# High and low input in one 512-column matmul, in half chunks of 256 channels

## The chip, the cores and the metric

The kernel runs on one core of a Trainium2 chip. The metric is the device time of one execution in microseconds. TensorE (PE) multiplies, with its weight loads (PEld) beside it; VectorE (DVE) and ScalarE (ACT) do the elementwise work; GpSimd (POOL) and SyncE (SP) issue most of the DMAs.

## The reference, cut to what matters

Two layers over x of 256 tokens by 2048 channels. Each layer projects x by `w_in` to 7680 columns, which three mixers share; the mixers' outputs are gated, joined, projected by `w_out` and merged into x.

```python
proj = x @ w_in
aq, ak, av, ag, bq, bk, bv, bg, cu, cglu, cg = jnp.split(proj, IN_OFFSETS, axis=-1)
ya = diff_attention(aq, ak, av, bias_a, lam, ...) * silu(ag)      # 4 heads of 128
yb = dilated_attention(bq, bk, bv, bias_b) * silu(bg)             # 8 heads of 128
yc = conformer_conv(cu, cglu, ...) * silu(cg)                     # 512 channels, 31 taps
x = layer_norm(ALPHA * x + jnp.concatenate([ya, yb, yc], -1) @ w_out, ln_g, ln_b)
```

All of it is float32.

## The kernel before, in words

**Products.** TensorE multiplies in its rounded float32 format. To keep the precision, every factor is split in a high part (the value rounded) and a low part (the remainder), and a product is the sum of three: high by high, high by low, low by high (`mm3`, lines 220 to 223). x^T lies in SBUF as `xh` and `xl`, [128 channels, 16 k-tiles, 256 tokens] each.

**Weights.** The columns of `w_in`, `conv_pw` and `w_out` come in groups of 512 KB, either 2 k-tiles by 512 columns (rows of 2 KB in DRAM) or 4 k-tiles by 256 columns (rows of 1 KB). `Stream` (lines 104 to 167) loads them into 5 `wraw` buffers by DMAs from SP, and splits each: ACT copies the high part (line 154), DVE subtracts for the low part (line 155). There are 6 buffers for each part. `pump`, called after each group, issues the next split as soon as the count of buffers allows with a slack of one, so a split waits for TensorE to be done with a group five places ahead of it.

**Chunks.** A layer's projection runs in chunks of 512 columns, 8 groups each. Twelve of them (cglu, cu, ag, aq, ak, bg, bq, bk, bg, bq, bk, cg) come out with channels on partitions: `chunk_w` (line 225) takes the weights as the stationary operand, 128 columns at a time (4 blocks `b`), and streams 256 tokens, so a k-tile is 4 x 3 matmuls of 256 columns. The others (av, bv) and the output projection come out with tokens on partitions: `chunk_x` (line 241) takes x as the stationary operand and streams 512 weight columns. Both sum in `acc`, 4 KB per partition of PSUM, of which there are two.

**The way out.** `evac` copies `acc` to SBUF on ACT, with a scale where wanted. `gate` takes ACT's tanh of `acc` and then a DVE step that reads `acc` again. For ak, two ACT copies put the two partition halves into `kz`. For cglu and cu, tanh on ACT and a DVE product into `hpad`.

**Fillers.** All other work of the layer is cut in steps and hung on ticks (`at`, `tick`); one tick passes after each k-tile of a dense chunk. The 124 taps of the convolution per layer (line 473, DVE) start at the chunk ag, at first one on each tick; heads of the attentions (`a_head`, `b_head`) run their scores, softmax, transposes and outputs on fixed ticks, among them small matmuls in TensorE's queue. Engines work through their queues in the order of the program.

Of the kernel before, what the change touches and what calls it, by code (L numbers as in the profile page):

```python
# [9 lines left out]
F32 = mybir.dt.float32  # L10
# [6 lines left out]
S = 256  # L17
# [4 lines left out]
CW = 31  # L22
# [19 lines left out]
def kernel(  # L42
# [32 lines left out]
    def u4(name, dt=F32):  # L75
        return work.tile([128, 1024], dt, tag="u4", name=name, bufs=N_U4)
# [3 lines left out]

    xh = big.tile([128, KT, S], F32R, name="xh")
    xl = big.tile([128, KT, S], F32R, name="xl")
    yh = big.tile([128, KT, S], F32R, name="yh")
# [16 lines left out]

# [1 line left out]
    groups = []  # L102

    class Stream:
# [33 lines left out]
        def split_part(self, i):  # L138
            """The two parts of group 0, which arrive one by one."""
            if i == 0:  # L140
                self.tiles(0)
            r, h, l = self.raw[0][:, i], self.hi[0][:, i], self.lo[0][:, i]
            nc.scalar.copy(h, r)
            nc.vector.tensor_tensor(l, r, h.bitcast(F32), OP.subtract)
            if i == 1:
                self.raw.pop(0)
                self.ns = 1
# [35 lines left out]
    for l in range(DEPTH):  # L183
        p = {}
        w = w_in[l]
        if l == 0:
            p["av"] = add_groups(w, OFF["av"], 512, KALL, 2)
        else:
            p["av0"] = add_groups(w, OFF["av"], 256, KALL, 4)
            p["av1"] = add_groups(w, OFF["av"] + 256, 256, KALL, 4)  # L190
        for c, o in (("cglu", 0), ("cu", 0), ("ag", 0), ("aq", 0), ("ak", 0),
                     ("bv", 0), ("bg", 0), ("bq", 0), ("bk", 0),
                     ("bv", 512), ("bg", 512), ("bq", 512), ("bk", 512), ("cg", 0)):
            p[c, o // 512] = add_groups(w, OFF[c] + o, 512, KALL, 2)
        p["pw"] = add_groups(conv_pw[l], 0, 512, list(range(4)), 2)
        for n in range(3):
            p["o", n] = add_groups(w_out[l], n * 512, 512, KOUT0 if n == 0 else KALL, 2)
        p["o3a"] = add_groups(w_out[l], 1536, 256, KALL, 4)
        p["o3b"] = add_groups(w_out[l], 1792, 256, KALL, 4)
        plan.append(p)  # L200

# [1 line left out]
    ticks = deque()  # L203
# [14 lines left out]

# [1 line left out]
    def mm3(o, ah, al, bh, bl, start, stop, skip=False):  # L220
        nc.tensor.matmul(out=o, lhsT=ah, rhs=bh, start=start, stop=False, skip_group_check=skip)  # L221
        nc.tensor.matmul(out=o, lhsT=ah, rhs=bl, start=False, stop=False, skip_group_check=skip)  # L222
        nc.tensor.matmul(out=o, lhsT=al, rhs=bh, start=False, stop=stop, skip_group_check=skip)  # L223

    def chunk_w(ids, mh, ml, nk=KT):
# [32 lines left out]
    def half_steps(ids, mh, ml, t, o, gi):  # L258
        """The products of one token tile with one group of a 256-column half."""
        ts = slice(t * 128, (t + 1) * 128)  # L260
# [5 lines left out]

# [1 line left out]
    def stage_y(kt, y):  # L268
# [6 lines left out]
    def b_head(h, q, k, v, g, t0):  # L275
        """Stages of one head of mixer B; h is its number, q, k, v, g its chunk's tiles."""
        j = h % 4
# [157 lines left out]

# [1 line left out]
    def gate(acc, name):  # L437
        t = u4(name)
        tv = v4(t, 4)
        nc.scalar.activation(tv, acc, AF.Tanh, scale=0.5)  # L440
        nc.vector.scalar_tensor_tensor(tv, tv, 1.0, acc, OP.add, OP.mult)
        return tv

    def evac(acc, name, scale=None):
        t = v4(u4(name), 4)
        if scale is None:
            nc.scalar.copy(t, acc)
        else:
            nc.scalar.activation(t, acc, AF.Copy, scale=scale)
        return t  # L450

# [4 lines left out]

# [1 line left out]
    def conv_start(l, acc_u, tg):  # L458
        """hpad <- 2 * cu * sigmoid(cglu); tg holds tanh(cglu / 2)."""
        nc.vector.scalar_tensor_tensor(hpad[:, :, CW - 1:], tg, 1.0, acc_u, OP.add, OP.mult)  # L460

# [86 lines left out]

# [1 line left out]
    class Norm:  # L550
        """r holds alpha * x + y by column chunk: [128 tokens, 2 token tiles, 512]."""

# [21 lines left out]
        def add(self, t, h, ps):  # L574
            """Column half h (256 wide) of token tile t."""
            r = self.r[h // 2][:, t, (h % 2) * 256:(h % 2 + 1) * 256]
            nc.vector.scalar_tensor_tensor(r, r, ALPHA, ps, OP.mult, OP.add)
            nc.vector.bn_stats(self.bn[t][:, h, :], r)
# [41 lines left out]

# [1 line left out]
    xr = [v4(u4("xr"), 4) for i in range(4)]  # L622
# [97 lines left out]

# [1 line left out]
    def enter(N, step):  # L722
        """Layer norm into x^T, the first chunk's products by token tile between: step(t, gi)."""
        def norm(t, *ns):
# [52 lines left out]

# [1 line left out]
    prev = None  # L779
    for l in range(DEPTH):  # L780
# [3 lines left out]
        else:  # L784
# [19 lines left out]
            av = avt  # L804
        acc = chunk_w(P["cglu", 0], xh, xl)
        tg = v4(u4("tg"), 4)
        nc.scalar.activation(tg, acc, AF.Tanh, scale=0.5)
        acc = chunk_w(P["cu", 0], xh, xl)
        conv_start(l, acc, tg)
        cd = {}  # L810
# [8 lines left out]
        conv_tail(l, cd, 166)  # L819
        ag = gate(chunk_w(P["ag", 0], xh, xl), "ag")  # L820
        aq = evac(chunk_w(P["aq", 0], xh, xl), "aq", 1.0 / 8.0)
        acc = chunk_w(P["ak", 0], xh, xl)
        nc.scalar.copy(kz[0:64, :, 0, :], acc[0:64])
        nc.scalar.copy(kz[64:128, :, 1, :], acc[64:128])
        for h in range(AH):
            a_head(l, h, aq, av, ag, 1 + 15 * h)
        sB = float(HD) ** -0.5
        for c in range(2):
            bv = evac_v(chunk_x(P["bv", c], xh, xl, KALL), "bv")
            bg = gate(chunk_w(P["bg", c], xh, xl), "bg")  # L830
            bq = evac(chunk_w(P["bq", c], xh, xl), "bq", sB)
            bk = evac(chunk_w(P["bk", c], xh, xl), "bk")
            for h in range(4):
                b_head(4 * c + h, bq, bk, bv, bg, 1 + (15 if c == 0 else 6) * h)
        acc = chunk_w(P["cg", 0], xh, xl)
        cg = gate(acc, "cg")
        acc = chunk_w(P["pw"], cd["hh"], cd["hl"], nk=4)
        for b in range(4):
            y = ytile()
            nc.vector.scalar_tensor_tensor(y, acc[:, b, :], 0.25, cg[:, b, :], OP.mult, OP.mult)  # L840
            stage_y(12 + b, y)
        # output projection
        N = Norm(l)
# [60 lines left out]
def _shape_consts():  # L904
    """One-hot buckets and window masks per distance 255 - m, and the identity and its mirror: functions of the shapes alone."""
    import numpy as np
# [46 lines left out]
```

## Time and profile before

| | us |
|---|---|
| median of 3 runs | 958.03 |
| lowest and highest of them | 957.79, 958.13 |
| span of the profiled execution, first to last instruction | 956.7 |
| TensorE busy | 936.8 |
| DVE busy | 636.5 |
| ACT busy | 438.2 |

The profile gives the profiled execution by its span alone. A busy TensorE is not TensorE at its peak: matmuls overlap, and the profile models their ends. The spacing of their starts tells what one costs in a stream. PEclk is the granted share of TensorE's full clock, in tenths.

### The profile page before, as it was taken

Reading aid. Unit: us, or ns where it says so; the run is one execution under the profiler, and the core shown is the slowest. Engines: PE = TensorE matmul, PEld = TensorE weight load, DVE = VectorE, ACT = ScalarE, POOL = GpSimd, SP = SyncE. Lnnn points to the kernel's source line nnn. Section 1 sums busy time; section 2 is a strip of 40 time slices with the busy share of each in tenths; the row PEclk is TensorE's granted clock in tenths of the full one; section 3 lists DMA queues with packets and bytes.
Section 4 is the critical chain, followed back from the end, with each engine's and each line's share of the span. In section 5 each row is a group of like instructions: output and inputs, shape, how many; then the busy total and the mean of one; then the engine's idle time right before and its main releaser. Section 6 shows DMA issues by size and latency. Waiting matters only on the chain. (4 is left out here: it accounts for less than half of the span.)

```text
span 956.7 us, 16597 instructions
## 1 busy us (share of the span) xinstructions
PE 936.8 (98%) x6710; PEld 881.0 (92%) x6710; DVE 636.5 (67%) x1030; ACT 438.2 (46%) x623; POOL 58.1 (6%) x78
## 2 busy tenths in 40 slices
PE   7999999999999999999999999999999999999995
PEld 5999998999999999888989999989998999998894
DVE  5657777676767567656765477767776676766556
ACT  5553345454544456433354433455455444654331
POOL 2100000000000000200240000000000000010004
PEclk9999999999999999999999999999999999999998
DMA  9956665555665555976457666665656655568632
GB/s 319 336 161 189 186 181 175 158 173 155 182 180 165 170 163 177 297 231 192 139 202 238 180 182 190 178 176 156 176 156 175 177 168 163 163 224 285 199 99 88
DMA packets 96285, 179.44 MB, mean 188 GB/s; under 512 B 5928, under 2 KB 18496, under 8 KB 96208
## 3 DMA queue, kind: packets, MB, share of 16 engines
q1 hardware_dynamic: 92096, 165.17, 56.4%
q0 software_dynamic: 3824, 12.68, 4.4%
q8 instruction: 52, 0.85, 0.4%
q10 hardware_dynamic: 288, 0.52, 0.1%
q14 instruction: 25, 0.20, 0.1%
HBM read 174.14 MB, written 4.21 MB: 186 GB/s over the span
## 5 line engine op out<-in xcount | busy, mean ns | idle before, releaser
L155 DVE TENSOR_TENSOR wlo<-wraw,whi 128x1024 fp32r<-128x1024 f32 x307 | 374.4, 1223 | 210.9 <-ACT whi L154 209.8
L154 ACT CAST whi<-wraw 128x1024 fp32r<-128x1024 f32 x307 | 320.5, 1049 | 296.7 <-PE acc L222 166.0
L221 PE MATMUL acc<-xh,whi 128*128 128x256 f32 x1536 | 442.2, 288 | 0.0
L223 PE MATMUL acc<-xh,wlo 128*128 128x256 f32 x1536 | 434.6, 283 | 0.0
L222 PE MATMUL acc<-xl,whi 128*128 128x256 f32 x1536 | 434.5, 283 | 0.0
L221 PEld LDWEIGHTS acc<-xh,whi 128*128 128x128 f32 x1536 | 294.6, 192 | 2.1 <-issue 1.4
L222 PEld LDWEIGHTS acc<-xl,whi 128*128 128x128 f32 x1536 | 294.5, 192 | 2.1 <-issue 1.4
L223 PEld LDWEIGHTS acc<-xh,wlo 128*128 128x128 f32 x1536 | 294.3, 192 | 0.0
L473 DVE SCALAR_TENSOR_TENSOR cacc<-hpad,cwh,cacc 128x256 f32<-128x256 f32 x240 | 115.4, 481 | 2.4
L221 PE MATMUL acc<-whi,yh 128*128 128x512 f32 (+1 forms) x256 | 93.8, 366 | 0.0
L223 PE MATMUL acc<-whi,yl 128*128 128x512 f32 (+1 forms) x256 | 92.9, 363 | 0.0
L222 PE MATMUL acc<-wlo,yh 128*128 128x512 f32 (+1 forms) x256 | 92.8, 363 | 0.0
L221 PE MATMUL acc<-whi,xh 128*128 128x512 f32 (+1 forms) x192 | 74.1, 386 | 1.6 <-ACT whi L154 1.0
L222 PE MATMUL acc<-wlo,xh 128*128 128x512 f32 (+1 forms) x192 | 71.9, 375 | 2.0 <-DVE wlo L155 1.5
L223 PE MATMUL acc<-whi,xl 128*128 128x512 f32 (+1 forms) x192 | 71.8, 374 | 0.0
L223 PEld LDWEIGHTS acc<-whi,yl 128*128 128x128 f32 x256 | 48.3, 189 | 7.7
L222 PEld LDWEIGHTS acc<-wlo,yh 128*128 128x128 f32 x256 | 48.4, 189 | 7.5
L221 PEld LDWEIGHTS acc<-whi,yh 128*128 128x128 f32 x256 | 48.3, 189 | 7.3
L221 PEld LDWEIGHTS acc<-whi,xh 128*128 128x128 f32 x192 | 36.2, 189 | 10.0 <-ACT whi L154 1.8
L222 PEld LDWEIGHTS acc<-wlo,xh 128*128 128x128 f32 x192 | 36.2, 189 | 9.3 <-DVE wlo L155 2.1
L223 PEld LDWEIGHTS acc<-whi,xl 128*128 128x128 f32 x192 | 36.2, 188 | 6.6
L410 POOL TENSOR_TENSOR sa<-sa,mhalf 128x2 f32<-128x2 f32 x8 | 5.8, 725 | 431.4 <-DVE sa L409 431.4
(175 smaller groups left out, 661.1 us busy)
## 6 DMA issues: line engine op xcount, KB each, us to landing
wraw<-in_w_in_dram SPq DMA_DIRECT2D x239, 512.0 KB, 4.3
wraw<-in_w_out_dram SPq DMA_DIRECT2D x64, 512.0 KB, 4.9
wraw<-in_conv_pw_dram SPq DMA_DIRECT2D x4, 512.0 KB, 4.4
rt<-in_x_dram POOLq DMA_DIRECT2D x4, 512.0 KB, 6.9
gb<-in_ln_g_dram POOLq DMA_DIRECT2D x8, 256.0 KB, 7.3
gb<-in_ln_b_dram POOLq DMA_DIRECT2D x8, 256.0 KB, 8.1
x_mid<-rt POOLq DMA_DIRECT2D x8, 256.0 KB, 7.1
rt<-x_mid POOLq DMA_DIRECT2D x4, 512.0 KB, 7.1
```

Of the source, the lines that this page charges most:

```text
L154: nc.scalar.copy(h, r)
L155: nc.vector.tensor_tensor(l, r, h.bitcast(F32), OP.subtract)
L221: nc.tensor.matmul(out=o, lhsT=ah, rhs=bh, start=start, stop=False, skip_group_check=skip)
L222: nc.tensor.matmul(out=o, lhsT=ah, rhs=bl, start=False, stop=False, skip_group_check=skip)
L223: nc.tensor.matmul(out=o, lhsT=al, rhs=bh, start=False, stop=stop, skip_group_check=skip)
L410: nc.gpsimd.tensor_tensor(m[:, 24:26], m[:, 22:24], mhalf[:, 0:2], OP.pow)
L473: nc.vector.scalar_tensor_tensor(a, h, w, a, OP.mult, OP.add)
```

## The change: what it does

- `xh` and `xl` become the two halves of one tile `xx`, [128, 16, 2, 256], so that the high and the low input of a k-tile lie side by side.
- The twelve chunks with channels on partitions run in two halves of 256 columns each. Their weights come in groups of 4 k-tiles by 256 columns, in rows of 1 KB.
- In `half_w`, for each k-tile and block, one matmul streams `xx[:, k]`, 512 columns, past the high weights into two parts of `acc` (high input, low input), and one of 256 columns streams the high input past the low weights into the second part. A tick passes after every second k-tile.
- `whole` sums the two parts on the way out: ACT copies the second part to SBUF, DVE adds the first from PSUM. `gate` works on that sum, with tanh and product on later ticks; `evac`, `conv_start` and `kz` use `whole` too.

The core of the diff (lines that only lose a comment are left out):

```diff
-    xh = big.tile([128, KT, S], F32R, name="xh")
-    xl = big.tile([128, KT, S], F32R, name="xl")
+    xx = big.tile([128, KT, 2, S], F32R, name="xx")
+    xh, xl = xx[:, :, 0, :], xx[:, :, 1, :]
...
-            p[c, o // 512] = add_groups(w, OFF[c] + o, 512, KALL, 2)
+            if c == "bv":
+                p[c, o // 512] = add_groups(w, OFF[c] + o, 512, KALL, 2)
+            else:
+                p[c, o // 512] = [add_groups(w, OFF[c] + o + 256 * j, 256, KALL, 4) for j in range(2)]
...
+    def half_w(ids, m2, nk=KT):
+        acc = acc_tile().rearrange("p (b i) s -> p b i s", b=2)
+        k = 0
+        for g in ids:
+            wh, wl = st.get(g)
+            for kk in range(nk // len(ids)):
+                for b in range(2):
+                    cs = slice(b * 128, (b + 1) * 128)
+                    nc.tensor.matmul(out=acc[:, b], lhsT=wh[:, kk, cs], rhs=m2[:, k], start=k == 0, stop=False,
+                                     skip_group_check=True)
+                    nc.tensor.matmul(out=acc[:, b, 1], lhsT=wl[:, kk, cs], rhs=m2[:, k, 0], start=False,
+                                     stop=k == nk - 1, skip_group_check=True)
+                k += 1
+                if k % 2 == 0:
+                    tick()
+            st.done(g)
+            st.pump()
+        return acc
...
-    def gate(acc, name):
-        t = u4(name)
-        tv = v4(t, 4)
-        nc.scalar.activation(tv, acc, AF.Tanh, scale=0.5)
-        nc.vector.scalar_tensor_tensor(tv, tv, 1.0, acc, OP.add, OP.mult)
+    def whole(z, acc, scale=None, c=slice(0, 128)):
+        if scale is None:
+            nc.scalar.copy(z, acc[c, :, 1])
+            nc.vector.tensor_tensor(z, acc[c, :, 0], z, OP.add)
+        else:
+            nc.scalar.activation(z, acc[c, :, 1], AF.Copy, scale=scale)
+            nc.vector.scalar_tensor_tensor(z, acc[c, :, 0], scale, z, OP.mult, OP.add)
+
+    def gate(ids, m2, name):
+        tv = v4(u4(name), 4)
+        for j in range(2):
+            z = tv[:, 2 * j:2 * j + 2, :]
+            whole(z, half_w(ids[j], m2))
+            d = {}
+
+            def s0(z=z, d=d):
+                d["t"] = work.tile([128, 768], F32, tag="s", name="s", bufs=3)[:, 0:512].rearrange(
+                    "p (b s) -> p b s", b=2)
+                nc.scalar.activation(d["t"], z, AF.Tanh, scale=0.5)
+
+            def s1(z=z, d=d):
+                nc.vector.scalar_tensor_tensor(z, d["t"], 1.0, z, OP.add, OP.mult)
+
+            at(1, s0)
+            at(2, s1)
         return tv
 
-    def evac(acc, name, scale=None):
...
+    def evac(ids, m2, name, scale=None):
+        tv = v4(u4(name), 4)
+        for j in range(2):
+            whole(tv[:, 2 * j:2 * j + 2, :], half_w(ids[j], m2), scale)
+        return tv
...
-        nc.vector.scalar_tensor_tensor(hpad[:, :, CW - 1:], tg, 1.0, acc_u, OP.add, OP.mult)
+    def conv_start(l, P):
+        tg = v4(u4("tg"), 4)
+        for j in range(2):
+            z = tg[:, 2 * j:2 * j + 2, :]
+            whole(z, half_w(P["cglu", 0][j], xx))
+            nc.scalar.activation(z, z, AF.Tanh, scale=0.5)
+        for j in range(2):
+            z = hpad[:, 2 * j:2 * j + 2, CW - 1:]
+            whole(z, half_w(P["cu", 0][j], xx))
+            nc.vector.scalar_tensor_tensor(z, tg[:, 2 * j:2 * j + 2, :], 1.0, z, OP.add, OP.mult)
...
-        acc = chunk_w(P["ak", 0], xh, xl)
-        nc.scalar.copy(kz[0:64, :, 0, :], acc[0:64])
-        nc.scalar.copy(kz[64:128, :, 1, :], acc[64:128])
+        ag = gate(P["ag", 0], xx, "ag")
+        aq = evac(P["aq", 0], xx, "aq", 1.0 / 8.0)
+        for j in range(2):
+            acc = half_w(P["ak", 0][j], xx)
+            for c in range(2):
+                ps = slice(64 * c, 64 * c + 64)
+                whole(kz[ps, 2 * j:2 * j + 2, c, :], acc, c=ps)
```

`bg`, `bq`, `bk` and `cg` change in the same way. `chunk_w` stays for `conv_pw` alone.

## Rows read from the trace of the kernel before

**Rows 1.** The page: busy time of each engine, and granted clock in 40 slices
```profile
PE 936.8 (98%) x6710; PEld 881.0 (92%) x6710; DVE 636.5 (67%) x1030; ACT 438.2 (46%) x623; POOL 58.1 (6%) x78
...
PEclk9999999999999999999999999999999999999998
```

**Rows 2.** Waits of TensorE and its weight loads, whole span (total, times, longest)
```profile
PE acc L264 <- ACT xh L615: 2.2, 3, 1.4
...
PE acc L264 <- DVE xl L619: 0.3, 1, 0.3
...
PEld acc L221 <- issue: 2.6, 9, 0.6
...
PEld aux L321 <- ACT pt L315: 0.7, 2, 0.3
```

**Rows 3.** Groups by line and shape: busy us, mean ns | idle before
```profile
L221 PE MATMUL acc<-xh,whi 128*128 128x256 f32 x1536 | 442.2, 288 | 0.0
```

**Rows 4.** Timeline of TensorE, chunk ag of layer 1 (start, length): first, last of 192
```profile
552.14 0.28 PE L221 MATMUL acc<-xh,whi 128*128 128x256 f32 x1
...
575.07 0.28 PE L223 MATMUL acc<-xh,wlo 128*128 128x256 f32 x1
```

**Rows 5.** Timeline of TensorE, output projection of layer 0: first and last of 192
```profile
408.27 0.39 PE L221 MATMUL acc<-whi,yh 128*128 128x512 f32 x1
...
451.56 0.39 PE L223 MATMUL acc<-whi,yl 128*128 128x512 f32 x1
```

**Rows 6.** Groups by line and shape: ACT and DVE at these widths
```profile
L619 DVE TENSOR_TENSOR xl<-aux,xh 128x512 fp32r<-128x512 f32 x8 | 5.4, 686 | 3.1 <-ACT xh L615 2.9
...
L441 DVE SCALAR_TENSOR_TENSOR bg<-bg,acc 128x1024 f32<-128x1024 f32 x4 | 4.9, 1221 | 5.6 <-ACT bg L440 5.6
...
L615 ACT CAST xh<-aux 128x512 fp32r<-128x512 f32 x8 | 4.6, 578 | 0.0
...
L447 ACT COPY bk<-acc 128x1024 f32<-128x1024 f32 x4 | 4.1, 1016 | 8.6 <-PE acc L223 8.6
...
L603 DVE SCALAR_TENSOR_TENSOR rt<-rt,mv,gb 128x512 f32<-128x512 f32 x3 | 4.0, 1341 | 0.2
```

**Rows 7.** Stretches: length, busy PE, PEld, DVE, ACT, POOL, clock, DMA share, GB/s
```profile
103.00:126.00 23.00, 23.00 (x194) 23.00 (x193) 17.64 (x25) 9.26 (x10) 0.00 (x0) 1.00 0.62 184
195.00:218.00 23.00, 23.00 (x188) 22.47 (x188) 18.29 (x37) 11.65 (x25) 0.70 (x1) 1.00 0.56 166
...
900.00:920.00 20.00, 20.00 (x90) 16.57 (x89) 11.48 (x15) 8.26 (x8) 0.00 (x0) 1.00 0.60 184
920.00:930.00 10.00, 10.00 (x79) 9.69 (x78) 7.81 (x12) 3.33 (x4) 0.00 (x0) 1.00 0.01 3
```

**Rows 8.** Waits of ACT's weight split, whole span
```profile
ACT whi L154 <- PE acc L222: 166.0, 102, 2.7
...
ACT whi L154 <- PE acc L223: 92.4, 60, 1.8
```

**Rows 9.** Timeline, end of chunk ak in layer 0: start, us, engine
```profile
148.60 1.05 ACT L154 CAST whi<-wraw 128x1024 fp32r<-128x1024 f32 x1 [1.83 <-PE acc L222]
...
149.68 1.23 DVE L155 TENSOR_TENSOR wlo<-wraw,whi 128x1024 fp32r<-128x1024 f32 x1 [0.74 <-ACT whi L154]
...
151.65 1.01 ACT L823 COPY kz<-acc 64x1024 f32<-64x1024 f32 x1 [2.01 <-PE acc L223]
152.68 1.01 ACT L824 COPY kz<-acc 64x1024 f32<-64x1024 f32 x1
...
154.15 0.59 PE L339 MATMUL aux<-kz,aq 128*128 128x256 f32 x2
```

**Rows 10.** Timeline: a softmax scaled, its transposes; a late weight load
```profile
306.39 0.35 DVE L305 TENSOR_SCALAR s<-s,st 128x256 f32<-128x256 f32 x1
...
309.81 0.49 PE L311 MATMUL aux<-ident,s 128*128 128x128 f32 x3
...
388.73 0.30 PEld L321 LDWEIGHTS aux<-pt,bv 128*128 128x128 f32 x2 [0.34 <-ACT pt L315]
```

More of the change, by code (lines that the diff above doesn't have):

```diff
@@ L434, in a_head @@
             at(t0 + i, f)
-    def gate(acc, name):
-        t = u4(name)
-        tv = v4(t, 4)
-        nc.scalar.activation(tv, acc, AF.Tanh, scale=0.5)
-        nc.vector.scalar_tensor_tensor(tv, tv, 1.0, acc, OP.add, OP.mult)
-        return tv
-    def evac(acc, name, scale=None):
[L445 to L450, printed above, removed]
+    def whole(z, acc, scale=None, c=slice(0, 128)):
[19 more added lines that the diff above has]
+            at(2, s1)
+        return tv
+    def evac(ids, m2, name, scale=None):
[3 more added lines that the diff above has]
+        return tv
     def evac_v(acc, name):
@@ L455, in evac_v @@
         return t
-    def conv_start(l, acc_u, tg):
-        nc.vector.scalar_tensor_tensor(hpad[:, :, CW - 1:], tg, 1.0, acc_u, OP.add, OP.mult)
+    def conv_start(l, P):
[8 more added lines that the diff above has]
+            nc.vector.scalar_tensor_tensor(z, tg[:, 2 * j:2 * j + 2, :], 1.0, z, OP.add, OP.mult)
     def conv_taps(l, d):
@@ L804 @@
             av = avt
[L805 to L809, printed above, removed]
+        conv_start(l, P)
         cd = {}
@@ L819 @@
         conv_tail(l, cd, 166)
-        ag = gate(chunk_w(P["ag", 0], xh, xl), "ag")
-        aq = evac(chunk_w(P["aq", 0], xh, xl), "aq", 1.0 / 8.0)
-        acc = chunk_w(P["ak", 0], xh, xl)
-        nc.scalar.copy(kz[0:64, :, 0, :], acc[0:64])
-        nc.scalar.copy(kz[64:128, :, 1, :], acc[64:128])
+        ag = gate(P["ag", 0], xx, "ag")
[5 more added lines that the diff above has]
+                whole(kz[ps, 2 * j:2 * j + 2, c, :], acc, c=ps)
         for h in range(AH):
@@ L829 @@
             bv = evac_v(chunk_x(P["bv", c], xh, xl, KALL), "bv")
-            bg = gate(chunk_w(P["bg", c], xh, xl), "bg")
-            bq = evac(chunk_w(P["bq", c], xh, xl), "bq", sB)
-            bk = evac(chunk_w(P["bk", c], xh, xl), "bk")
+            bg = gate(P["bg", c], xx, "bg")
+            bq = evac(P["bq", c], xx, "bq", sB)
+            bk = evac(P["bk", c], xx, "bk")
             for h in range(4):
                 b_head(4 * c + h, bq, bk, bv, bg, 1 + (15 if c == 0 else 6) * h)
-        acc = chunk_w(P["cg", 0], xh, xl)
-        cg = gate(acc, "cg")
+        cg = gate(P["cg", 0], xx, "cg")
         acc = chunk_w(P["pw"], cd["hh"], cd["hl"], nk=4)
```

## The prediction

> **What bounds the kernel now.** I read the busy shares and the clock first, then what TensorE waited for, then the spacing of its matmuls. TensorE is busy 98% of the span, at the full one of its two clocks (2.4 GHz) in all slices but the last [rows 1], but that share alone says little, since matmul ends are modelled. The waits say more: the eight rows of TensorE's own waits add up to 7.9 us in 956.7, nearly all at the start and at the change of layer [rows 2]. The first and the last of the eight stand in the rows, with two of the weight loads' waits. So whatever shortens TensorE's stream shortens the run, and what slows another engine costs nothing until it makes TensorE wait.
>
> The stream itself: 3 x 1536 products of 256 columns come from `chunk_w`; one of the three alike groups stands in [rows 3]. In a chunk with no attention work between, 192 such matmuls start from 552.14 to 575.07, 22.93 / 191 = 0.1200 us each [rows 4]. The 512-column products of the output projection run 192 starts from 408.27 to 451.56, 43.29 / 191 = 0.2267 us each [rows 5]. The difference, 0.1067 us for 256 more columns, is 2.4 columns per ns, the full clock; what is left, 0.1200 - 0.1067 = 0.0133 us, is paid per matmul whatever its width. Every matmul in both streams has its own weight load, and in most pairs of neighbours the weights differ or are loaded again, so this fixed part already contains the change of weights.
>
> **The change, part by part.**
>
> *The products.* In 12 chunks of each layer, for each of 16 k-tiles and 4 blocks, three 256-column products (high by high, high by low, low by high) become one of 512 and one of 256. Columns stay 768; one matmul and one weight load go. Before: 3 x 0.1200 = 0.3600. After: 0.2267 + 0.1200 = 0.3467. Saved: 0.0134 us in each of 12 x 2 x 16 x 4 = 1536 places (the count of the group in [rows 3]), together 20.6 us; with the spacings unrounded 20.7. The trace has no stream that alternates 512 and 256 columns. Bounds: the pair can't be under its columns' time, 0.320, and at worst the wide product costs as much as the two it replaces, 0.360. I take 0.3467, since both widths show the same fixed part and the weight load for the wide product falls behind a 256-column product exactly as all do in [rows 4].
>
> On that fixed part the Trainium skill says otherwise ("TensorE: Matmul & The Clock Gate", Back-to-back issue gap): a warm matmul is spaced by its columns at 2.4 GHz plus about 2.5 ns. By it the saving would be only 1536 x 2.5 ns = 3.8 us. The rows here show 13.3 ns [rows 4, 5], at both widths, so I go by the rows.
>
> *The stream of weights.* A group stays 512 KB, but its rows in DRAM become 1 KB instead of 2 KB, with twice the packets for the same number of DMA issues on SP's queue. The last eight groups of the program are already such groups (256 columns): 0.60 of the DMA engines' time gave 184 GB/s at 900 to 920, which is 3.7 MB, seven of the eight groups, and after 920 almost nothing is left [rows 7]. That is 307 GB/s for a full share, against 184 / 0.62 = 297 with 2 KB rows at 103 to 126 [rows 7]. Cost: nothing. A group lasts 8 x 0.3467 = 2.77 us on TensorE, so the stream must give 189 GB/s, a share of 0.62.
>
> *The way out of PSUM.* Where one ACT copy of 128x1024 (1.016 us) or the gate's ACT plus DVE pair (DVE 1.221) emptied a chunk, each half now takes an ACT copy of 128x512 and a DVE add [rows 6]. The nearest rows are 0.578 for a 128x512 ACT cast from PSUM and 0.686 for a 128x512 DVE tensor_tensor from PSUM [rows 6]. DVE gains per layer: five plain chunks 5 x 1.37 = 6.9; four gates 4 x (1.37 + 0.15) = 6.1; cglu 1.4; cu 1.5; ak, whose two partition halves are added apart, 4 x 0.69 = 2.7. That is 18.6 per layer, 37 in all, on 636.5 [rows 1]: 72% of a span of 936. ACT gains about 18 on 438. The scaled adds and the gate's scalar_tensor_tensor at 128x512 have no row: bounds 0.61 (half of 1.221) and 1.34 (the slowest of that shape), I take 0.69, because 1.221 reads PSUM as they do [rows 6].
>
> What covers this is the lead of the weight split. ACT's split waits for TensorE to release a buffer, 166.0 + 92.4 us in all [rows 8]: it runs as far ahead as six buffers allow. With a slack of one that is five groups, 5 x 24 x 0.120 = 14.4 us, less the two split steps 1.05 and 1.23 [rows 9]: about 12.1 us in hand. In the densest stretch of the taps DVE still stands idle 0.74 us in each group, waiting for ACT [rows 9]. A new add holds DVE until the half's last matmul and ACT's copy are done (0.58), then takes 0.69; behind it wait taps, the next low split and the heads' softmax steps, all of which TensorE needs later. Per half: 17.64 / 23 x 11.5 = 8.8 us of DVE with half a gate of 0.61 in it [rows 7], plus 0.69 for the add and 0.69 - 0.61 for the gate, makes 9.6 in a half of 32 x 0.3467 = 11.1 us. Should DVE reach the add early, it stands still from its last low split, 1.05 + 1.23 after a group's end, to 0.58 after the next one's: 2.77 + 0.58 - 2.28 = 1.07. Even then 10.7 fits, and the lead is not needed.
>
> *The small matmuls of the heads* stand in TensorE's queue at fixed ticks, so a late DVE or ACT step there stops the whole stream. A softmax row is scaled at 306.39 and done at 306.74; its transposes start at 309.81, 3 us later [rows 10]. At the one place where a copy came late the weight load waited 0.34 us [rows 10], 0.7 us in both layers together [rows 2]. For kz the margin is small: its last copy ends at 153.69, the first scores start at 154.15 [rows 9]. Now ACT copies at about 151.65 and 152.25 (0.58 each), DVE adds to about 153.7: the same margin, and head 0 needs only the first half, which is ready 11 us earlier. Bounds for new waits: none, or 0.34 at each of 24 heads, 8.2 us. I take 0.7, the same small wait once more.
>
> *High and low input in one tile.* Should the waits treat the interleaved halves as one region, the first products after the change of layer would wait for the low part as well: eight steps of up to 0.69 us (the add's twin row, [rows 6]), 5.5 us. That place now waits 2.2 us for the high part [rows 2], and the low part's own wait is seen separately there. I take nothing and keep 5.5 as the bound.
>
> **The sum.** Span 956.7 - 20.7 + 0.7 = 936.7. The median of the runs shown, 958.03, is 1.3 above this execution's span, and the program's ends are untouched: 938.0 us.
>
> **The rivals.**
> A. As summed, 938.0; own range 935 to 942. Below 938: no new wait (937.3), and the 2.6 us in which weight loads of the high products waited for nothing that shows [rows 2] gone with them, 934.7; above, new waits of up to 5 us.
> B. New waits at half boundaries or at the change of layer eat a part: 0.34 at every head (8.2 us) or 5.5 us at the change, together up to 13.7: 942 to 951. For it: in-order queues and 48 halves where there were 24 chunks. Against it: 3 us margins in [rows 10].
> C. The wide product brings nothing, because alternating widths expose the weight change: pair at 0.360, 956.7 + 0.7 + 1.3 = 958.7, no change. Against it: the fixed part is the same at both widths.
> D. Little of the fixed part is saved, because most of it belongs to the columns and not to the matmul: were four fifths of the 20.7 a price per column, which the 768 columns keep, it would be 936.7 + 16.5 + 1.3 = 954.5. Against it: a price per column would be twice as large at 512, and [rows 4, 5] show the same at both widths. By the 2.5 ns of the Trainium skill, cited above, the time would be 956.7 - 3.8 + 0.7 + 1.3 = 954.9.
> E. Slower: DVE becomes the bound at the half boundaries. Take the fullest window, 18.29 / 23 x 11.5 = 9.15 us per half [rows 7], both new DVE steps at the slow 1.34 (less the 0.61 of gate already there) and 1.07 of standing still: 12.3 us against TensorE's 11.1, 1.2 late in each of 48 halves, 58 us, less 12.1 of lead in each layer: 33 us, 936.0 + 33 + 1.3 = 970. It decides from about 12.0 us of DVE per half on, where (12.0 - 11.1) x 48 - 24 eats the 20.7. Against it: most of the adds are tensor_tensor, whose row is 0.69, and a DVE that is late doesn't stand still.
>
> **How the numbers follow.** Chances: A 0.82, B 0.08, C 0.04, D 0.02, E 0.04. A change within 0.2% (1.9 us) can't be told from none on this kernel. A, B and D are faster: 0.92. C lies within 0.2%, with a part of it just beyond on the slow side: same 0.03; slower 0.05. The range, 935 to 946, takes in A and the 8.2 us bound of B without the change of layer, and leaves out 0.05 of B's cases with C, D and E, under 0.2 in all.
>
> **What would show it.** Right: wide starts 0.227 us before the narrow one and narrow 0.120 before the next wide; a half chunk of 32 pairs in 11.1 us; 1536 fewer dense matmuls; DMA share near 0.62 with 1 KB rows; DVE near 673 us busy; TensorE's waits still under 10 us. Wrong: a pair at 0.36 (C) or at 0.357 (D); rows of TensorE waiting for whi or wlo in the middle of a layer (E); new rows of TensorE waiting for pt, s or kz, or longer ones for xl at the change of layer (B).

## The result, and the profile after

The changed kernel takes 946.18 us, the median of four runs (944.15, 945.92, 946.45, 946.55), against 957.91 for the kernel before in the same comparison. The ratio is 0.987, with an interval of 0.9859 to 0.9882. The forecast was 938.0, in a range that ends at 946.0: the sign was right, the gain was 11.7 us instead of 20, and the median lies 0.2 us above the range's upper end. The profiled execution, the fastest of the four, took 944.15 us with a span of 942.4.

The page after, busy times and clock, answers to [rows 1]; below them the two groups of products that took the place of the three of [rows 3]:

```profile
PE 923.2 (98%) x5174; PEld 798.2 (85%) x5174; DVE 668.6 (71%) x1092; ACT 452.9 (48%) x671; POOL 58.1 (6%) x78
...
PEclk9999999999999999999999999999999999999998
...
L239 PE MATMUL acc<-xx,whi 128*128 128x512 f32 x1536 | 549.3, 401 | 0.0
...
L241 PE MATMUL acc<-xx,wlo 128*128 128x256 f32 x1536 | 430.2, 280 | 0.0
```

TensorE runs 6710 - 5174 = 1536 matmuls fewer, at the full clock as before. DVE came to 668.6 us (673 forecast), ACT to 452.9 (456).

TensorE's waits, whole span (total, times, longest), answer to [rows 2]:

```profile
PE acc L289 <- ACT xx L668: 2.2, 3, 1.4
...
PE acc L289 <- DVE xx L672: 0.3, 1, 0.3
...
PEld aux L346 <- ACT pt L340: 0.7, 2, 0.3
```

All eight rows of TensorE's own waits add up to 7.4 us (7.9 before), and the largest of them, the one at the change of layer and the weight loads' wait for `pt` are what they were. No wait for `whi` or `wlo` appears in the middle of a layer, none for `s` or `kz`. So nothing new stops the stream, and what the change gave or failed to give is in the spacing of the products.

That spacing, from the starts of the pairs in the profiled execution ("wide" is the product of 512 columns, "narrow" the one of 256): 0.2341 us from a wide product to the narrow one, 0.1166 from the narrow one to the next wide one, 0.3507 for the pair. It leaves out 54 of the 1536 pairs, whose wide product starts right behind a head's small matmuls and is followed by the narrow one only after 0.31 to 0.64 us (the kernel before has 54 such places too). What all the pairs gave stands between the first product of cglu in layer 0 and TensorE's last row, first before the change, then after it:

```profile
33.47 0.28 PE L221 MATMUL acc<-xh,whi 128*128 128x256 f32 x1
...
944.20 0.64 PE L264 MATMUL acc<-whi,yl 128*128 128x256 f32 x4
```

```profile
32.92 0.39 PE L239 MATMUL acc<-xx,whi 128*128 128x512 f32 x1
...
930.04 0.64 PE L289 MATMUL acc<-whi,yl 128*128 128x256 f32 x4
```

910.73 us became 897.12, 13.6 less. The other 0.7 of the span's 14.3 us lie almost all ahead of these rows, where the start took 0.55 us less in this execution. The gain is uneven: ag, aq and ak of layer 0 went from 23.04 us to 22.19 each, 13.3 ns a pair as forecast; the quiet chunks of layer 1, cglu to ak, from 23.04 to 22.61, some 6.7 ns a pair; the chunks with the heads' work gained 6.4 to 10.3. The mean of all 1536 pairs is 8.9 ns.

So 0.3507 is a mean, and in the stretches without heads' work it is one over two rhythms. Layer 0, chunk aq, timeline of TensorE (start, length): the first two products of a half, and its last wide one:

```profile
102.88 0.39 PE L239 MATMUL acc<-xx,whi 128*128 128x512 f32 x1
103.11 0.28 PE L241 MATMUL acc<-xx,wlo 128*128 128x256 f32 x1
...
113.62 0.39 PE L239 MATMUL acc<-xx,whi 128*128 128x512 f32 x1
```

31 pairs in 10.74 us are 0.3465 each: the forecast, to the resolution of these rows. The same view, layer 1, inside chunk ag:

```profile
544.99 0.40 PE L239 MATMUL acc<-xx,whi 128*128 128x512 f32 x1
545.24 0.28 PE L241 MATMUL acc<-xx,wlo 128*128 128x256 f32 x1
545.36 0.40 PE L239 MATMUL acc<-xx,whi 128*128 128x512 f32 x1
545.59 0.28 PE L241 MATMUL acc<-xx,wlo 128*128 128x256 f32 x1
545.70 0.40 PE L239 MATMUL acc<-xx,whi 128*128 128x512 f32 x1
545.94 0.28 PE L241 MATMUL acc<-xx,wlo 128*128 128x256 f32 x1
546.05 0.40 PE L239 MATMUL acc<-xx,whi 128*128 128x512 f32 x1
```

Here three pairs of 0.37, 0.34 and 0.35 us take 1.06 us together, 0.3533 each, and this repeats through the half. No wait stands in either stretch, the code is the same line, the shapes are the same. In the undisturbed halves each rhythm keeps itself up: 0.3533 in cglu of layer 0, 0.3467 from the second half of cu to ak there, 0.3533 in all of cglu to ak of layer 1. The fast one is the sum of the two steady spacings, 0.2267 + 0.1200, though the width changes at every product; the slow one is 6.6 ns over it. Where the heads' small matmuls stand between (bg to cg), the two mix.

The steps out of PSUM, groups by line and shape, answer to [rows 6]:

```profile
L469 DVE SCALAR_TENSOR_TENSOR bq<-acc,bq 128x512 f32<-128x512 f32 x8 | 5.5, 692 | 3.9 <-ACT bq L468 3.8
...
L466 DVE TENSOR_TENSOR bk<-acc,bk 128x512 f32<-128x512 f32 x8 | 5.5, 686 | 5.7 <-ACT bk L465 5.7
...
L485 DVE SCALAR_TENSOR_TENSOR bg<-s,bg 128x512 f32<-128x512 f32 x8 | 5.5, 684 | 0.0
...
L465 ACT COPY bk<-acc 128x512 f32<-128x512 f32 x8 | 4.7, 587 | 15.7 <-PE acc L241 15.7
```

The scaled add and the gate's product, which had no row before, take 0.692 and 0.684 (0.69 taken), ACT's copy 0.587 (0.578 taken).

Two windows (length, busy PE, PEld, DVE, ACT, POOL, clock, DMA share, GB/s) answer to [rows 7], and ACT's waits in front of its weight split to [rows 8]:

```profile
103.00:126.00 23.00, 23.00 (x135) 20.25 (x134) 18.23 (x28) 10.66 (x13) 0.00 (x0) 1.00 0.69 199
543.00:600.00 57.00, 57.00 (x325) 49.37 (x324) 45.88 (x68) 24.52 (x28) 0.00 (x0) 1.00 0.63 184
```

```profile
ACT whi L154 <- PE acc L226: 91.3, 59, 1.8
ACT whi L154 <- PE acc L239: 74.3, 53, 1.8
```

With rows of 1 KB the DMA engines move 199 / 0.69 = 288 and 184 / 0.63 = 292 GB/s for a full share, against 297 with 2 KB: too little to matter with a third of the share free. And ACT still waits often for TensorE to free a buffer, 165.6 us in these two rows where it was 258.4: the lead of the split, which was to cover DVE's additions, is still there.

The end of chunk ak in layer 0 (start, length, engine), against [rows 9]:

```profile
148.06 0.68 DVE L466 TENSOR_TENSOR kz<-acc,kz 64x512 f32<-64x512 f32 x1 [0.69 <-ACT kz L465]
148.78 0.58 ACT L465 COPY kz<-acc 64x512 f32<-64x512 f32 x1 [0.75 <-DVE kz L466]
149.39 0.69 DVE L466 TENSOR_TENSOR kz<-acc,kz 64x512 f32<-64x512 f32 x1 [0.65 <-ACT kz L465]
150.02 0.59 PE L364 MATMUL aux<-kz,aq 128*128 128x256 f32 x2
```

ACT's second copy did not follow the first at once, as I had it: it stood 0.75 us, at a semaphore of the program, until DVE's first add was done. So the last add ends at 150.08, after the scores began at 150.02. It cost nothing: the scores' row has no wait, and head 0 needs just the first half of `kz`.

### The profile page after: what moved, and what is told of

Its sections match the earlier page's. It is cut to its first block, busy times and chain, and to the rows that moved or that the text cites. A ratio compares the mean times of both kernels' runs of the same rounds, so it can differ in the third digit from the quotient of the medians.

```text
span 942.4 us, 13625 instructions
## 1 busy us (share of the span) xinstructions
PE 923.2 (98%) x5174; PEld 798.2 (85%) x5174; DVE 668.6 (71%) x1092; ACT 452.9 (48%) x671; POOL 58.1 (6%) x78
## 5 line engine op out<-in xcount | busy, mean ns | idle before, releaser
L239 PE MATMUL acc<-xx,whi 128*128 128x512 f32 x1536 | 549.3, 401 | 0.0
L241 PE MATMUL acc<-xx,wlo 128*128 128x256 f32 x1536 | 430.2, 280 | 0.0
L239 PEld LDWEIGHTS acc<-xx,whi 128*128 128x128 f32 x1536 | 288.4, 188 | 68.3 <-issue 1.0
L241 PEld LDWEIGHTS acc<-xx,wlo 128*128 128x128 f32 x1536 | 290.0, 189 | 2.1 <-issue 1.4
L224 PE MATMUL acc<-whi,xx 128*128 128x512 f32 (+1 forms) x192 | 74.1, 386 | 1.1 <-ACT whi L154 0.7
L225 PE MATMUL acc<-wlo,xx 128*128 128x512 f32 (+1 forms) x192 | 71.9, 374 | 2.0 <-DVE wlo L155 1.5
L226 PE MATMUL acc<-whi,xx 128*128 128x512 f32 (+1 forms) x192 | 71.8, 374 | 0.0
L224 PEld LDWEIGHTS acc<-whi,xx 128*128 128x128 f32 x192 | 36.2, 189 | 9.6 <-ACT whi L154 1.6
L225 PEld LDWEIGHTS acc<-wlo,xx 128*128 128x128 f32 x192 | 36.2, 189 | 9.3 <-DVE wlo L155 2.1
L226 PEld LDWEIGHTS acc<-whi,xx 128*128 128x128 f32 x192 | 36.2, 188 | 6.6
L294 ACT CAST yh<-y 128x256 fp32r<-128x256 f32 x32 | 12.9, 405 | 30.0 <-DVE y L351 10.9
L630 DVE SCALAR_TENSOR_TENSOR rt<-rt,acc 128x256 f32<-128x256 f32 x32 | 13.1, 410 | 13.5 <-PE acc L289 7.1
```

Of the source, the lines that this page charges most:

```text
L239: nc.tensor.matmul(out=acc[:, b], lhsT=wh[:, kk, cs], rhs=m2[:, k], start=k == 0, stop=False, skip_group_check=True)
L241: nc.tensor.matmul(out=acc[:, b, 1], lhsT=wl[:, kk, cs], rhs=m2[:, k, 0], start=False, stop=k == nk - 1, skip_group_check=True)
L294: nc.scalar.copy(yh[:, kt, :], y)
```

## The experiments

The question is why a pair costs 0.3507 us in the mean and not 0.3467, what the rest of the change costs, and whether the missing part can be had. My theory is that the change of width between neighbours costs something on TensorE. The rivals: the place in PSUM where the narrow product adds; the halves, adds and 1 KB rows; a weight load that only just fits behind 256 columns; the place of the buffers. The first four kernels ran side by side on one chip (before 958.30), the next four on a second (958.16), the last two on a third (958.13).

**The wide product taken apart again (e1_three256).** Everything of the change stays, but each wide product is two of 256 columns.

```diff
-                    nc.tensor.matmul(out=acc[:, b], lhsT=wh[:, kk, cs], rhs=m2[:, k], start=k == 0, stop=False,
+                    nc.tensor.matmul(out=acc[:, b, 0], lhsT=wh[:, kk, cs], rhs=m2[:, k, 0], start=k == 0, stop=False,
+                                     skip_group_check=True)
+                    nc.tensor.matmul(out=acc[:, b, 1], lhsT=wh[:, kk, cs], rhs=m2[:, k, 1], start=False, stop=False,
```

> The changed kernel with halves, 1 KB rows, ticks, two parts and adds as they are, but the wide product taken apart again into two of 256 columns. If only the matmuls' spacing decides: 3 x 0.120 us per place as before the change, so 957 to 959 us, no change against the kernel before. If halves, adds or 1 KB rows cost TensorE time that the gain hid (about 6 us of the 20.7 forecast are missing): 962 to 965.

Measured: 958.25 us, ratio 0.9997 (0.9988 to 1.0006). TensorE's timeline, layer 1, eight products apart:

```profile
551.93 0.28 PE L239 MATMUL acc<-xx,whi 128*128 128x256 f32 x1
...
552.89 0.28 PE L243 MATMUL acc<-xx,wlo 128*128 128x256 f32 x1
```

0.96 / 8 = 0.120 us each, as in [rows 4]. The 24 chunks together take what they take in the kernel before, to 0.01 us. So half chunks, adds, 1 KB rows, ticks and one tile for both inputs cost nothing together, and the whole gain comes from the joined product. Changing the weights costs nothing of its own in a stream of one width either: this one still takes `whi`, `whi`, `wlo` in turn.

**The narrow product adds into the first part (e2_part0).** Same sum, other place.

```diff
-                    nc.tensor.matmul(out=acc[:, b, 1], lhsT=wl[:, kk, cs], rhs=m2[:, k, 0], start=False,
+                    nc.tensor.matmul(out=acc[:, b, 0], lhsT=wl[:, kk, cs], rhs=m2[:, k, 0], start=False,
```

> The narrow product adds into the first part of the sum instead of the second; all else as changed. If the pair is slow because the narrow product writes columns that the wide one has only just written: every pair at 0.3467 us, 938 to 940. If the alternation of widths makes it slow, whatever is written where: the two patterns stay (0.3467 and 0.353), 944 to 947.

Measured: 946.01 us, ratio 0.9868 (0.9855 to 0.9882), the time of the changed kernel. The place is not it. The same half of aq in layer 0 as above, first and last wide product:

```profile
103.11 0.40 PE L239 MATMUL acc<-xx,whi 128*128 128x512 f32 x1
...
114.08 0.40 PE L239 MATMUL acc<-xx,whi 128*128 128x512 f32 x1
```

10.97 / 31 = 0.354: the slow rhythm, in a stretch where the profiled execution of the changed kernel had the fast one. One of this kernel's four runs took 944.37, the others 945.78 to 946.26, as those of the changed kernel are 944.15 and 945.92 to 946.55. Between the two profiled executions (spans 944.5 here, 942.4 there) seven undisturbed halves of 32 pairs at the slower rhythm make 7 x 32 x 0.0066 = 1.5 of the 2.1 us; the first half chunk also starts 0.7 us later here (33.60 against 32.92). Whether the unprofiled runs differ by the same, they don't show, and the last experiment but two (e8) has a profile where it is otherwise.

**Two wide, two narrow (e3_wide_wide).** For each k-tile the two wide products of both blocks, then the two narrow ones: half as many changes of width.

```diff
                                      skip_group_check=True)
+                for b in range(2):
+                    cs = slice(b * 128, (b + 1) * 128)
                     nc.tensor.matmul(out=acc[:, b, 1], lhsT=wl[:, kk, cs], rhs=m2[:, k, 0], start=False,
```

> Per k-tile both wide products first, then both narrow ones: the same matmuls, half as many changes of width. If the change of width costs: wide after wide 0.227, narrow after narrow 0.120, and 941 to 944. If the place of the sum costs (it is now written 227 ns later): 938 to 940. If halves and adds cost: no change, 946.

Measured: 941.42 us, ratio 0.9823 (0.9809 to 0.9836). The five runs took 941.12, 941.12, 941.42, 941.55 and, once, 3262.11 us, for which no profile shows the reason. In the timeline, where neighbours of a group are one row (x2), the second of these rows of wide products is the 40th after the first:

```profile
567.80 0.63 PE L239 MATMUL acc<-xx,whi 128*128 128x512 f32 x2
...
595.67 0.62 PE L239 MATMUL acc<-xx,whi 128*128 128x512 f32 x2
```

27.87 / 80 = 0.3484 us a pair. Reordering alone, with the same products and weights, gives back 4.8 us, so time is lost where the widths alternate. The total came as expected of a price for each change of width, the spacing did not: from wide to wide it is 0.233, not 0.227. And such a price is not what the rows show. This order holds 0.3483 in every undisturbed half of both layers, 5 ns under the slow rhythm but 1.7 ns over the fast one, which changes width twice as often.

**Eight wide, eight narrow (e4_by_group).** All wide products of a group of weights, then its narrow ones.

```diff
+            for lo in range(2):
+                for kk in range(n):
+                    for b in range(2):
...
+                        if lo == 0:
+                            nc.tensor.matmul(out=acc[:, b], lhsT=wh[:, kk, cs], rhs=m2[:, k + kk],
...
+                        else:
+                            nc.tensor.matmul(out=acc[:, b, 1], lhsT=wl[:, kk, cs], rhs=m2[:, k + kk, 0],
...
+                    if (lo, kk) in ((0, 2), (1, 3)):
+                        tick()
```

> Per group of 4 k-tiles all eight wide products, then all eight narrow ones: two changes of width in 16 matmuls instead of 16. If the change of width costs: 0.2267 and 0.1200 nearly everywhere, 938 to 940. If streaming the interleaved input costs: wide products above 0.227 here too, and 944 or more. If halves and adds cost: 946.

Measured: 942.18 us, ratio 0.9832 (0.9819 to 0.9845). Timeline, layer 1:

```profile
545.20 2.00 PE L242 MATMUL acc<-xx,whi 128*128 128x512 f32 x8
547.03 1.12 PE L245 MATMUL acc<-xx,wlo 128*128 128x256 f32 x8
547.99 2.00 PE L242 MATMUL acc<-xx,whi 128*128 128x512 f32 x8
...
570.34 2.00 PE L242 MATMUL acc<-xx,whi 128*128 128x512 f32 x8
```

Nine rounds of eight pairs take 25.14 us, 0.3492 a pair. The narrow run takes 0.96 / 8 = 0.120 each, the steady value; the wide run 1.83 / 8 = 0.229, over it. From one start to the next its eight wide products take 233, 236, 228, 233, 230, 227, 227 and 226 ns, the last three at the steady 226.7. So streaming the interleaved input costs nothing by itself, and the price is not one lump at the change: the spacing settles over some five products. That would be why a run of eight is no better than a run of two. The 938 to 940 expected of two changes in 16 products was missed by 2 us.

**A wider narrow product (e5_narrow384).** It streams 384 columns, which adds low by low for half the tokens. Nothing but the width changes.

```diff
-                    nc.tensor.matmul(out=acc[:, b, 1], lhsT=wl[:, kk, cs], rhs=m2[:, k, 0], start=False,
+                    nc.tensor.matmul(out=af[:, b, 0:384], lhsT=wl[:, kk, cs], rhs=mf[:, k, 0:384], start=False,
```

> The narrow product streams 384 columns instead of 256 (it also takes low by low for half of the tokens), so 128 more in 1536 places; order as in the changed kernel. Without any excess a pair is 0.2267 + 0.1733 = 0.4000 us, which is 938.0 + 1536 x 0.0533 = 1020 us. If the weight load for the wide product only just fits behind 256 columns and makes the excess: no excess here, 0.400 and 1019 to 1021. If any change of width brings the excess of 4 to 6.6 ns a pair: 1026 to 1031, with wide products at 0.230 to 0.241.

Measured: 1036.68 us, ratio 1.0817 (1.0802 to 1.0832). Timeline in layer 1:

```profile
599.81 0.40 PE L241 MATMUL acc<-xx,whi 128*128 128x512 f32 x1
600.05 0.34 PE L243 MATMUL acc<-xx,wlo 128*128 128x384 f32 x1
600.22 0.40 PE L241 MATMUL acc<-xx,whi 128*128 128x512 f32 x1
...
600.64 0.40 PE L241 MATMUL acc<-xx,whi 128*128 128x512 f32 x1
```

0.83 / 2 = 0.415 in these rows; over whole undisturbed halves 0.4133 in layer 1, 0.4067 in layer 0; 0.4105 in the mean of all but the 54 pairs right behind small matmuls. Two steady streams would give 0.2267 + 0.1733 = 0.4000, and the run about 938 + 1536 x 0.0533 = 1020. Were a weight load that only just fits behind 256 columns the cause, the excess would have gone with 128 columns more to load behind. It grew, from 4.0 to 10.5 ns a pair. That theory falls; of the change of width the kind was right and my figure (1026 to 1031) too small.

**Four and four (e6_four_four).** The order of e4 over two k-tiles at a time.

```diff
+            for kk in range(0, nk // len(ids), 2):
+                for lo in range(2):
+                    for q in range(2):
+                        for b in range(2):
```

> Per two k-tiles four wide products, then four narrow ones: a change of width after every fourth matmul. If each change costs a settling of the spacing: between the orders of two and of eight, 941 to 942.5. If what matters is only that no wide product stands alone: at or below the order of two, 940 to 941.5.

Measured: 943.76 us, ratio 0.9851 (0.9837 to 0.9864); 0.351 us a pair in the undisturbed halves. Both expectations missed: the gain doesn't follow the number of changes (two: 941.4, four: 943.8, eight: 942.2). Over the steady sum a whole cycle lost 3.4 ns with runs of two, 17 with four, 20 with eight. It looks as if a run of four pays nearly the full price of settling, twice as often as a run of eight; why a run of two pays so little, these rows don't tell.

**Sixteen and sixteen (e7_two_groups).** The wide products of two groups of weights, then their narrow ones. If the price is a fixed 20 ns for a run that settles, doubling the run from e4 should give about 1536 / 8 x 20 / 2 = 1.9 us.

```diff
+        for gp in range(0, len(ids), 2):
+            two = ids[gp:gp + 2]
+            ws = [st.get(g) for g in two]
+            for lo in range(2):
+                for q in range(2 * n):
+                    w = ws[q // n][lo]
...
+                    if (lo, q) in ((0, 2), (0, 5), (1, 1), (1, 7)):
+                        tick()
+                    if lo == 1 and q % n == n - 1:
+                        st.done(two[q // n])
+                        st.pump()
```

> Per two groups sixteen wide products, then sixteen narrow ones: half as many changes as in the order of eight. If the excess is paid per change: about 1.9 us under that order, 940 to 941. If buffers held longer make TensorE wait: 943 or more, with rows of waits for whi or wlo.

Measured: 941.03 us, ratio 0.9819 (0.9805 to 0.9832), with no new wait of TensorE. Timeline, layer 1:

```profile
547.88 3.82 PE L244 MATMUL acc<-xx,whi 128*128 128x512 f32 x16
551.53 2.08 PE L247 MATMUL acc<-xx,wlo 128*128 128x256 f32 x16
553.45 3.82 PE L244 MATMUL acc<-xx,whi 128*128 128x512 f32 x16
...
564.58 3.82 PE L244 MATMUL acc<-xx,whi 128*128 128x512 f32 x16
```

Three rounds of 16 pairs in 16.70 us are 0.3479 a pair; a cycle loses 20 ns, as with eight. The step from e4, which ran on another chip, was 1.15 us, of the sign of the estimate and some 60% of its size. With e3 this is the best version, 5 us under the changed kernel and 17 under the one before; e3 and e7 can't be told apart by their times (941.12 to 941.55 without the one long run, 940.30 to 941.50).

**Without the adds (e8_no_add).** `whole` only copies the first part; the second part of every sum is left out.

```diff
-            nc.scalar.copy(z, acc[c, :, 1])
-            nc.vector.tensor_tensor(z, acc[c, :, 0], z, OP.add)
+            nc.scalar.copy(z, acc[c, :, 0])
```

> The changed kernel without DVE's adds on the way out: only the first part is copied (the second part of every sum is left out). If the adds are hidden behind TensorE: 944 to 947, as with them. If they are the missing 6 us: 938 to 940.

Measured: 945.45 us, ratio 0.9867 (0.9854 to 0.9881), in two levels: 944.34, 944.38 and 946.52, 946.96. The lower level is that of the changed kernel's best run: without the adds nothing is faster. The profiled execution (946.52, span 944.7) says so more sharply: its 24 chunks together take what they take in the changed kernel's profile to within 0.1 us, the fast rhythm in the same seven halves. What it has more, it has ahead of them (a wait of TensorE, two windows as above, the first wide product):

```profile
PE acc L224 <- ACT whi L154: 2.0, 1, 2.0
...
10.00:15.00 5.00, 2.73 (x6) 1.83 (x7) 2.52 (x3) 2.65 (x5) 0.00 (x0) 0.64 0.97 330
15.00:20.00 5.00, 5.00 (x17) 4.01 (x16) 4.55 (x5) 4.16 (x7) 0.00 (x0) 0.68 1.05 407
...
35.40 0.39 PE L239 MATMUL acc<-xx,whi 128*128 128x512 f32 x1
```

TensorE waited 2.0 us for a weight group of the first chunk (0.7 in the changed kernel's profile), then for a while had the lower of its two clocks, 1.2 GHz (granted clock 0.64 and 0.68 in the mean of these windows, 1.00 there), and the first half chunk began at 35.40 and not 32.92, 2.5 us late. So here the upper level came from the start and not from the rhythm; the two lower runs have no profile.

**An extra product of 512 columns ahead of each half (e9_lead512).** It asks whether what runs just before a half sets the rhythm. Its result is overwritten.

```diff
+        nc.tensor.matmul(out=acc[:, 0], lhsT=m2[:, 0, 0, 0:128], rhs=m2[:, 0], start=True, stop=True,
+                         skip_group_check=True)
```

> One more matmul of 512 columns ahead of each half chunk (its sum is thrown away by the first real product), 48 x 0.227 = 10.9 us. If the repeating pattern is chosen by what ran just before: the halves of layer 1 without attention work, cglu to ak, that all ran at 353 ns a pair now run at another value, 346.7 if the extra matmul does what the bias matmuls of layer 0 did; 31 pairs then take 10.75 instead of 10.95 us in every such half, and the whole 947 to 955 us. If the pattern belongs to the place of the buffers in memory or to the weights: 353 there as before, 957 us.

Measured: 956.05 us, ratio 0.9979 (0.9969 to 0.9988). The 48 extra products cost 48 x 0.2267 = 10.9 us, so at unchanged rhythms it would be 957.1. The halves of layer 1 stay at 0.3531 a pair: the expectation missed, this lead does not redraw the rhythm there. In layer 0 one half changed, the second of cglu, from 0.3536 to 0.3469.

**The same with 128 columns (e10_lead128).**

```diff
+        nc.tensor.matmul(out=acc[:, 0, 0, 0:128], lhsT=m2[:, 0, 0, 0:128], rhs=m2[:, 0, 0, 0:128], start=True,
+                         stop=True, skip_group_check=True)
```

> The same with a matmul of 128 columns, 48 x 0.07 to 0.12 us, 3.4 to 5.8 us. If what ran before chooses the pattern, any of the values may come, and alike in all undisturbed halves; if the place does: 353 there, 949.5 to 952 us.

Measured: 950.51 us, ratio 0.992 (0.9905 to 0.9935). First and last wide product of two halves of layer 1, one behind the other:

```profile
547.29 0.45 PE L241 MATMUL acc<-xx,whi 128*128 128x512 f32 x1
...
558.29 0.40 PE L241 MATMUL acc<-xx,whi 128*128 128x512 f32 x1
...
558.71 0.45 PE L241 MATMUL acc<-xx,whi 128*128 128x512 f32 x1
...
569.51 0.39 PE L241 MATMUL acc<-xx,whi 128*128 128x512 f32 x1
```

11.00 / 31 = 0.3548, then 10.80 / 31 = 0.3484, and again 0.3552 in the next. These means hold one longer first step behind the small product; from the second wide product on they are the two rhythms again, 0.3533, 0.3467 and 0.3533, and through layer 1 one undisturbed half in three runs the fast one. The total fits what I expected of the place (949.5 to 952), but the halves fit neither expectation: they are not all 0.353, and not all alike. One small product, with all buffers in their old places, is enough to change the rhythm of some halves in a layer that had kept 0.3533 throughout. That speaks against the place of the buffers and for what TensorE did before, without showing how it is chosen.

## Why the prediction was right, and where its size was wrong

**The bound.** Right. TensorE's stream set the time: of the 14.3 us that the span fell by, 13.6 lie in that stream from the first half chunk on, the rest nearly all in the start.

**The products: the step that failed, in size.** The mechanism held: one fixed part per matmul goes. The term was "After: 0.2267 + 0.1200 = 0.3467", the sum of two streams that each keep one width. No row alternated them, and I took the sum because both widths show the same fixed part; that reason does not carry over to a stream that alternates. Measured 0.3507 in the profiled execution, and over all pairs 8.9 ns saved and not 13.4, 13.6 us and not 20.7. The bounds 0.320 and 0.360 held, and the first of the two rhythms is the forecast's value; I kept the bounds but gave too little weight to what lies between them. What I had named to show it, narrow 0.227 after wide and wide 0.120 after narrow, came as 0.234 and 0.117.

**From 938.0 to 946.18.** The stream 20.7 - 13.6 = +7.1; no new wait, -0.7; the start, -0.55; which makes the span 942.4 for 936.7, to 0.15. Around the span 944.15 - 942.4 = 1.75 and not 1.3, +0.45. The median over the profiled execution +2.0, of which these runs don't show the cause: in e2's profile 1.5 us of such a step were the slow rhythm in more halves, in e8's it was the start.

**The range.** The median lies 0.2 us above its upper end. That it comes so near owes something to luck: I had set the end at 946 for B, new waits, of which there are none, and the number falls within B's 942 to 951 by another way.

**The stream of weights, the way out of PSUM, the heads, one tile.** Right: nothing, nothing, nothing (0.7 taken), nothing. After shows no new wait; e1 keeps all of it and runs as the kernel before, and e8 leaves the adds out with no gain. The lead of ACT's split and DVE's idle time covered 32 us more of DVE. For kz the margin that I called the same was gone by 0.06 us; the reserve that I named, that head 0 needs only the first half, covered it.

**The rivals.** B (new waits) and E (DVE as the bound) did not occur: 7.4 us of waits, none inside a layer. C (pair at 0.360) is refuted, and so is D at its 954.5, though D had the sign of the error: part of the fixed time stays. The Trainium skill ("TensorE: Matmul & The Clock Gate", Back-to-back issue gap) gives a matmul at the full clock a spacing of its columns plus about 2.5 ns, and calls that the isolated gap. This case's streams don't agree: they stand 13.3 ns above their columns [rows 4, 5], and a removed matmul gave back 8.9 ns in the mean, 13.3 where the fast rhythm ran.

**What stays open.** Shown: the loss belongs to TensorE's stream of mixed widths (none in e1, where all are 256 wide), the order of the same products changes it, after a long narrow run it settles over some five products, and a small product ahead of the halves changes which rhythm some of them have. Not shown: a price per change of width, which the fast rhythm and the runs of four contradict; what inside the chip makes the spacing settle; and what picks the rhythm. All 32 wide products of a half ahead of its 32 narrow ones wasn't tried; it would hold four groups of weights at a time.

## What to carry to other kernels

Where TensorE sets the time, joining two matmuls that share their weights saves at most the fixed part of one, 13.3 ns here, and in this kernel's alternating stream between 6.4 and 13.3 ns by stretch; price an alternating stream from a stream that alternates, not from the sum of two that don't. Order products of different widths in runs and try several lengths, since two and sixteen were good and four was not: the order alone was worth 5 us of 946. Work on the other engines, 32 us more of DVE here, was free where the rows show a lead and no wait in the bottleneck's queue, and a kernel that leaves that work out shows it in one run.

## What the runs showed of the hardware that was not expected

- The same stream of 512 and 256 columns runs in two rhythms, 346.7 and 353.3 ns a pair, each of which keeps itself up for whole chunks; with 384 columns for 256 the two are 406.7 and 413.3. In both cases they lie 6.6 ns apart.
- After a run of narrow products the spacing of wide ones goes 233, 236, 228, 233, 230 ns before it stands at 227. Over the steady sum a cycle loses 3.4 ns with runs of two, 17 with four, 20 with eight and with sixteen.
- One program has two levels of time about 2 us apart (944.2 and 946.4; in e8 944.4 and 946.7). The profiles show two ways to such a step: the slow rhythm in seven more halves (e2, 1.5 us), and a start in which TensorE waited 2.0 us and then had the lower clock for a while (e8, 2.5 us).
